# Sums of output weight blocks, made in the prompt's output stage and read back by the sample's

## The chip, the cores and the metric

The kernel runs on one core of a Trainium2 chip. The metric is device time in microseconds of one execution, and the median over runs is compared. TensorE (PE in the profile) multiplies matrices, VectorE (DVE) and GpSimd (POOL) work on elements, ScalarE (ACT) applies functions and copies, and SyncE (SP) issues the transfers between DRAM and the on-chip memory (SBUF). Results of TensorE land in PSUM, in 8 banks.

## The reference

One encoder layer is applied with the same weights to two batches, the prompt (512 tokens) and the sample (1024 tokens), 1024 channels wide, all in float32.

```python
def encoder_layer(x, norm_g, w_in, ..., w_o_a, w_o_b, w_out, t5_table):
    h = rmsnorm(x, norm_g)
    proj = h @ w_in
    qa, ka, va, za, qb, kb, vb, zb, ga, gb = jnp.split(proj, ..., axis=-1)
    ...
    oa = neighbourhood_attention(qa, ka, va, rpb_a) * jax.nn.silu(za)
    oa = oa @ w_o_a
    ...
    ob = window_gqa_attention(qb, kb, vb, t5_table, sink_b) * jax.nn.silu(zb)
    ob = ob @ w_o_b
    merged = jax.nn.sigmoid(ga) * oa + jax.nn.sigmoid(gb) * ob
    return x + merged @ w_out
```

This case is about the last line, merged @ w_out, for the prompt and for the sample.

## The kernel before

**Matrix products.** Every float32 factor is split into a high and a low part (`split`: ScalarE makes the high part, VectorE or GpSimd the low one as a difference), and a product is three matmuls: high by high, high by low, low by high (lines 1288, 1289 and 1290). A weight tile of 128 x 512 holds four blocks of 128 x 128, that is four steps over k, so one `product` of a weight tile is 12 matmuls of 512 columns.

**Stages.** The order is: prompt attention, prompt dense stages, sample attention, sample dense stages. A dense phase runs through the gate products, the merge, and at last the output stage, which takes the 8 chunks of w_out's columns in 4 pairs. A pair has four raw weight tiles, written (m, j): chunk m of the pair, half j of k.

**The prompt's output stage** uses `pair_classic` (line 1312): for each chunk of a pair it loads two raw tiles (`load_raw`, line 1250), splits them (`weight_tiles`, line 1255), and makes two products into one bank. `post_out` (line 1566) adds x and stores y.

**The sample's output stage** uses Strassen-Winograd products on the pair, 7 products for 8, in `pairs_apart` (line 1401). They need sums of the weight tiles: s1 = (1,0) + (1,1), s2 = s1 - (0,0), s3 = (0,0) - (1,0), s4 = (0,1) - s2. A first loop over the four pairs loads the four raw tiles, makes the four sums in tiles named S, stores s1, s2 and s3 in DRAM (`s_d`, line 1430), and computes three products, with (0,0), (0,1) and s4. A second loop loads s1, s2 and s3 again (line 1452) along with the raw tile (1,1), and computes the other four. The first loop's weights are prepared while the merge (`merged_sums` and the lines around it) is still running.

**What sets the order.** A planner (`Flow.run`) works when the program is built. It simulates the engines with costs in nanoseconds, takes on each engine the ready operation of the lowest priority number, and so fixes the order in which each engine, and the DMA queue, gets its instructions. An addition of two SBUF tiles (`tt`, line 1161) may go to VectorE or GpSimd; the planner charges 602 ns on the one and 1249 ns on the other, and takes the engine that would be done first, with a bias. On the chip each engine then goes through its list and waits on semaphores.

**Rings.** A tile of a ring (`room`, line 233) is given out when the tile that many places before it is free, that is when every operation that names it is done. The rings of `IN_TURN` (line 153) are given out strictly in the order of the program. Those that matter here: "raw" (4 tiles, for loaded weights), "whi" and "wlo" (6 each, for split weights; the attention weights of the sample come next in the same rings), "S" (3, in the sample only), "C" (x and y).

**The hand-over.** The sample's attention opens its late tiles (line 1849) only when the pools of the prompt's output stage are released; "raw" and "C" are in them.

Of the kernel before, what the change touches and what calls it, by code (L numbers as in the profile page):

```python
# [10 lines left out]
F32 = mybir.dt.float32  # L11
F32R = mybir.dt.float32r
AF = mybir.ActivationFunctionType
ALU = mybir.AluOpType
# [26 lines left out]
P = 128  # L41
# [313 lines left out]
def encoder_kernel(  # L355
# [23 lines left out]
    nc = tc.nc  # L379
# [22 lines left out]
    r_d = dpool.tile([NT_S // P, P], F32, tag="r_d", name="r_d")  # L402
    t_d = dpool.tile([4, 4, P, NT_S // 2], F32, tag="t_d", name="t_d")
    o_d = {geo.nt: dpool.tile([2, 8, P, geo.nt], F32, tag=f"o_d{geo.nt}", name=f"o_d{geo.nt}") for geo in (gp, gs)}

    def expand(geo, h, lo):

# [728 lines left out]
    def dense_phase(geo, hh, hl, h_ops, o_stores, exps_done, start, opened, tp, up, p0, p1, p2, x_t, y_t, classic, fill, after_gates=None, side=None):  # L1136
# [3 lines left out]
        nh = 512  # L1140
# [3 lines left out]
        short = nt == nh  # L1144
# [2 lines left out]
        g_d = dpool.tile([2, 8, P, nt], F32, tag=f"g_d{nt}", name=f"g_d{nt}")  # L1147
        p_d = None if short else dpool.tile([2, 4, P, sn], F32, tag="p_d", name="p_d")
        m_d = None if short else dpool.tile([4, 4, P, sn], F32, tag="m_d", name="m_d")
        s_d = None if short else dpool.tile([8, 3, P, nh], F32, tag="s_d", name="s_d")  # L1150
        stores = {}
        h_reads = []
        tags = iter(ROTA * 50)
# [155 lines left out]

            return mov  # L1310

        def pair_classic(srcs, post, prio, mov_h, after=lambda i: ()):

            i = 0
            for m, src in enumerate(srcs):
                ws = weight_tiles([load_raw(src[j], prio - 2) for j in range(2)], 4, prio)
                for n in halves:
                    ps = bank(next(tags))
                    o = product(ps, ws[0], mov_h(0, n), prio, True, False, after(i))
                    h_reads.append(product(ps, ws[1], mov_h(1, n), prio, False, True, [o]))  # L1320
                    i += 1
                    post(m, n * nh, nh, ps, True, prio)
# [78 lines left out]
        def pairs_apart(jobs, prio, mov_h, mov_t, late, seed=None, ready=()):  # L1401

            kept = []

            def take(ps, w, mov, pr, first, last, after=(), again=False, n=sn):
                o = product(ps, w, mov, pr, first, last, [*after, *ready], n, again)
                h_reads.append(o)
                return o
# [3 lines left out]
                    (("act", ACT_(sn, False)),), lambda e: act.activation(out.t, ps.t[:, :sn], AF.Copy), pr, new=[out], use=[ps],  # L1412
                )

            for i, (at, srcs, post) in enumerate(jobs):
                pr = prio + i / 8
                raw = {(m, j): load_raw(srcs[m][j], pr - 2) for m, j in ((0, 0), (1, 0), (1, 1), (0, 1))}
                s1, s2, s4, s3 = (tile_("S", 3, 512) for _ in range(4))
                saves = []
                for j, out, in0, in1, op in (  # L1420
                    (2, s1, raw[1, 0], raw[1, 1], ALU.add), (0, s2, s1, raw[0, 0], ALU.subtract),
                    (None, s4, raw[0, 1], s2, ALU.subtract), (1, s3, raw[0, 0], raw[1, 0], ALU.subtract),
                ):
                    tt(
                        lambda out=out: out.t, lambda in0=in0: in0.t, lambda in1=in1: in1.t, op, 512,
                        pr - 0.5 + (j == 1), new=[out], use=[in0, in1],
                    )
                    if j is not None:
                        saves.append(dma(
                            lambda j=j, out=out, at=at: nc.sync.dma_start(s_d[at, j], out.t), 262144, pr, use=[out],  # L1430
                        ))
                w = weight_tiles([raw[0, 0], raw[0, 1], s4], 6, pr - 0.5)
                p1, c = (spare(t) for t in (("fr", "fl"), ("fr", "fl"), ("fh", "fc"), ("fh", "w32"))[i])
                ps, p7 = bank(next(tags)), bank(next(tags))
                take(ps, w[0], mov_h(0, 0), pr, True, True)
                o = leave(p1, ps, pr)
                take(p7, w[2], mov_h(1, 1), pr, True, True)
                if seed:
                    seed(i)(0, sn, sn, None, pr, c, ready)
                    tt(lambda c=c: c.t[:, :sn], lambda c=c: c.t[:, :sn], lambda p7=p7: p7.t[:, :sn], ALU.add, sn, pr, psum=True, use=[c, p7], into=[c])  # L1440
                else:
                    leave(c, p7, pr)
                take(ps, w[1], mov_h(1, 0), pr, False, True, [o], True)
                post(0, 0, sn, ps, True, pr)
                kept.append((p1, c, saves))

            for i, ((at, srcs, post), (p1, c, saves)) in enumerate(zip(jobs, kept)):
                pr = late + i
                raw = []
                for j in range(3):  # L1450
                    v = tile_("raw", 4, 512)
                    dma(lambda v=v, j=j, at=at: nc.sync.dma_start(v.t, s_d[at, j]), 262144, pr - 2, new=[v], after=saves)
                    raw.append(v)
                w = weight_tiles([*raw, load_raw(srcs[1][1], pr - 2)], 6, pr - 0.5)
                pv = lambda v: (lambda: v.t[:, :sn])

                def mul(j, t):
# [286 lines left out]
        mov_h = blocks(m_ops, nh)  # L1744
        if not short:
            jobs = [
                (4 + i, [[w_out[c, j] for j in range(2)] for c in (2 * i, 2 * i + 1)], lambda m, *a, i=i: post_out(2 * i + m, *a))
                for i in range(4)
            ]
            seeds = lambda i: lambda m, *a: with_x(2 * i + m, *a)  # L1750
# [3 lines left out]
        for i in range(4):  # L1754
            srcs = [[w_out[c, j] for j in range(2)] for c in (2 * i, 2 * i + 1)]
            post = lambda m, *a, i=i: post_out(2 * i + m, *a)
            if i < o_classic:
                pair_classic(srcs, post, 20 + i, mov_h)
            else:
                seed = lambda m, *a, i=i: with_x(2 * i + m, *a)  # L1760
                pair_strassen(srcs, post, 20 + i, mov_h, mov_t, seed, i == 3)
# [180 lines left out]
```

## Time and profile before

| What | Value |
|---|---|
| three runs | 1134.73, 1137.67, 1137.1 us; median 1137.1 |
| the profiled execution | 1136.88 us, its span 1135.1 us |
| granted TensorE clock | 1.00 over nearly all of the span |
| transfers | 186.11 MB, 164 GB/s in the mean |
| prompt's output stage, TensorE | 351.1 to 394.6 us from the start of the span |
| sample's output stage, TensorE | 1054.6 to 1131.9 us |

The profile shows one execution. Times in its rows count from the start of the span. A group's row gives the engine, the source line, the operation, the tile written and the tiles read, and how often; L1164 is the addition in `tt`, L1170 and L1175 are the two halves of `split`. A matmul's busy time (0.39 us for 512 columns) overlaps the next matmul's, so the start-to-start distance is what a matmul costs.

### The profile page before, as it was taken

The numbers are of one execution on the slowest core, as the hardware profiler recorded it, in microseconds if no ns is written. First come the engines' busy times: TensorE is split into PE (matmuls) and PEld (weight loads), VectorE is DVE, ScalarE is ACT, GpSimd is POOL, SyncE is SP. The second block draws the span as 40 slices with busy tenths as digits, with TensorE's granted clock in tenths as the row PEclk, the third lists the DMA queues.
The fourth block names the chain that finished last, engine by engine and source line by source line (L and its number), as shares of the span: only waits on it lengthen the run. The fifth ranks groups of instructions, "written<-read, shape, count | busy, mean of one in ns | idle before, by whom it ended". The sixth has DMA issues, their size and how long they took to land.

```text
span 1135.1 us, 18686 instructions
## 1 busy us (share of the span) xinstructions
PE 1121.6 (99%) x6079; PEld 973.9 (86%) x6079; DVE 863.8 (76%) x1995; ACT 653.7 (58%) x1498; POOL 327.1 (29%) x432
## 2 busy tenths in 40 slices
PE   8999999999999999999999999999999999999998
PEld 6999988888888889999899988988788888788887
DVE  5888797587765468887868888885888866779874
ACT  6777987644433246574759888876534434522440
POOL 4654433000010044433414344420033221124221
PEclk9999999999999999999999999999999999999999
DMA  7854533488786422121312314244958645868982
GB/s 261 273 157 139 183 115 103 110 262 260 241 276 196 159 91 72 29 79 29 91 32 84 82 38 112 57 131 127 300 187 244 218 167 180 297 219 281 302 279 93
DMA packets 139108, 186.11 MB, mean 164 GB/s; under 512 B 29897, under 2 KB 68561, under 8 KB 139010
## 3 DMA queue, kind: packets, MB, share of 16 engines
q1 hardware_dynamic: 139010, 184.91, 51.4%
q8 instruction: 48, 0.79, 0.3%
q14 instruction: 50, 0.41, 0.1%
HBM read 138.71 MB, written 50.88 MB: 167 GB/s over the span
## 4 chain that ended last, share of the span: by engine, by line
PE 89%; DMA 4%; DVE 4%; ACT 1%; issue 1%; SPq 0%; POOL 0%; DVEq 0%; POOLq 0%; ACTq 0%
PE p L761 25%; PE x L1288 8%; PE x L1290 8%; PE x L1289 8%; PE x L1063 5%; PE x L1026 5%; PE x L934 5%; PE d L1288 4%; PE d L1289 4%; PE d L1290 4%; PE p L1289 4%; PE p L1290 4%; PE p L1288 4%; PE x L861 2%; DMA ot<-u_d 1%
## 5 line engine op out<-in xcount | busy, mean ns | idle before, releaser
L761 PE MATMUL p<-whi,hh 128*128 128x384 f32 x384 | 133.6, 348 | 0.0
L761 PE MATMUL p<-whi,hl 128*128 128x384 f32 x384 | 132.4, 345 | 0.0
L761 PE MATMUL p<-wlo,hh 128*128 128x384 f32 x384 | 132.2, 344 | 0.0
L978 ACT ACTIVATE sb<-sb,mx 128x384 f32<-128x384 f32 (+1 forms) x192 | 107.7, 565 | 22.9 <-DVE mx L969 22.6
L1170 ACT ACTIVATE whi<-raw 128x512 fp32r<-128x512 f32 (+1 forms) x136 | 79.4, 599 | 67.4 <-PE x L1289 46.3
L1289 PE MATMUL x<-T,whi 128*128 128x512 f32 x284 | 110.7, 390 | 0.3 <-DVE T L1175 0.2
L1288 PE MATMUL x<-T,whi 128*128 128x512 f32 x284 | 110.6, 390 | 0.0
L1290 PE MATMUL x<-T,wlo 128*128 128x512 f32 x284 | 110.5, 389 | 0.0
L761 PE MATMUL p<-whi,hb 128*128 128x384 f32 x384 | 107.8, 346 | 0.0
L1037 DVE TENSOR_TENSOR pp<-x,pp 128x512 fp32r<-128x512 f32 (+1 forms) x136 | 82.6, 639 | 20.3 <-ACT pp L1032 19.2
L1175 DVE TENSOR_TENSOR wlo<-raw,whi 128x512 fp32r<-128x512 f32 (+1 forms) x109 | 73.3, 682 | 26.5 <-ACT whi L1170 26.0
L1175 POOL TENSOR_TENSOR wlo<-raw,whi 128x512 fp32r<-128x512 f32 (+1 forms) x27 | 32.1, 1199 | 172.9 <-ACT whi L1170 160.2
L799 POOL TENSOR_TENSOR rs_r<-rs_v,mhalf 128x4 f32<-128x4 f32 (+1 forms) x72 | 79.9, 1109 | 5.7
L1032 ACT ACTIVATE pp<-x 128x512 fp32r<-128x512 f32 (+1 forms) x136 | 70.9, 561 | 18.2 <-PE x L1026 17.1
L792 POOL TENSOR_SCALAR rs_v<-ss 128x4 f32<-128x4 f32 (+1 forms) x72 | 26.0, 361 | 185.1 <-DVE ss L785 181.7
L1063 PE MATMUL x<-pp,v 128*128 128x256 f32 (+1 forms) x368 | 76.6, 322 | 0.0
L1288 PE MATMUL x<-hh,whi 128*128 128x512 f32 x196 | 76.4, 390 | 0.1
L1290 PE MATMUL x<-hh,wlo 128*128 128x512 f32 x196 | 76.3, 389 | 0.0
L1289 PE MATMUL x<-hl,whi 128*128 128x512 f32 x196 | 76.2, 389 | 0.0
L761 PEld LDWEIGHTS p<-whi,hl 128*128 128x128 f32 x384 | 72.8, 190 | 1.3 <-issue 1.0
L761 PEld LDWEIGHTS p<-whi,hh 128*128 128x128 f32 x384 | 73.0, 190 | 1.1 <-issue 0.5
L761 PEld LDWEIGHTS p<-wlo,hh 128*128 128x128 f32 x384 | 72.9, 190 | 0.9 <-issue 0.5
(381 smaller groups left out, 3011.9 us busy)
## 6 DMA issues: line engine op xcount, KB each, us to landing
raw<-in_w_g_dram SPq DMA_DIRECT2D x84, 256.0 KB
w<-in_w_att_dram SPq DMA_DIRECT2D x46, 384.0 KB
raw<-in_w_z_dram SPq DMA_DIRECT2D x40, 256.0 KB
ot<-o_d SPq DMA_DIRECT2D x36, 256.0 KB
raw<-in_w_out_dram SPq DMA_DIRECT2D x36, 256.0 KB
g_d<-C SPq DMA_DIRECT2D x34, 256.0 KB
fr<-in_w_g_dram SPq DMA_DIRECT2D x28, 256.0 KB
out_dram<-C SPq DMA_DIRECT2D x19, 256.0 KB
```

The costliest lines, as they stand in the source:

```text
L761: pe.matmul(ps.t[:, :GW], part[u](k), mv.t[:, c], start=k == 0 and m == 0, stop=k == KC - 1 and m == 2,)
L799: lambda e: nc.gpsimd.tensor_tensor(r.t[:, :nn], rv.t[:, :nn], mhalf[:, :nn], op=ALU.pow),
L934: pe.matmul(pss[2 * pair + i].t[:, :width], q.t[rows, u, at : at + P], kv[:, tiles[0] : tiles[-1] + 1 : step], start=n == 0, stop=n == 2,)
L978: act.activation(sb.t[:, :width], sb.t[:, :width], AF.Exp, bias=mx.t[:, i : i + 1], scale=-1.0, accum_out=sm.t[:, i : i + 1],)
L1032: lambda e, pt=pt, pp=pp, nn=nn: act.activation(pp.t[:, 0, :nn], pt.t[:, :nn], AF.Copy),
L1037: lambda e, pt=pt, pp=pp, nn=nn: dve.tensor_tensor(pp.t[:, 1, :nn], pt.t[:, :nn], pp.t[:, 0, :nn].bitcast(F32), op=ALU.subtract),
L1063: pe.matmul(out(), v.t[:, vs], mv(), start=first, stop=last)
L1170: (("act", ACT_(n)),), lambda e: act.activation(hi(), src(), AF.Copy), prio,
L1175: lambda e: engines[e].tensor_tensor(lo(), src(), hi().bitcast(F32), op=ALU.subtract), prio,
L1288: pe.matmul(out, hi.t[:, cs], mh(), start=first and k == 0, stop=False, **more)
L1289: pe.matmul(out, hi.t[:, cs], ml(), start=False, stop=False, **more)
L1290: pe.matmul(out, lo.t[:, cs], mh(), start=False, stop=last and k == len(ws) - 1, **more)
```

## The change

The sums move to the prompt's output stage. `weight_sums` is called there once per pair, after the pair's last split is planned. It waits for all of the pair's splits and then makes the four sums in a chain, each one in place of a raw tile that has been split: s1 into (1,1), s3 into (1,0), s2 into (0,0), s4 into (0,1). Each is stored in `s_d`, which is now one DRAM tile for the whole kernel and holds four sums a pair.

In the sample, the first loop loads (0,0), (0,1) and s4, and the second s1, s2, s3 and (1,1). No S tiles are made there and nothing is stored in `s_d`. A load of a sum waits for its own store only.

```diff
+    s_d = dpool.tile([4, 4, P, 512], F32, tag="s_d", name="s_d")
+    s_saves = {}
...
-        s_d = None if short else dpool.tile([8, 3, P, nh], F32, tag="s_d", name="s_d")
...
-        def pair_classic(srcs, post, prio, mov_h, after=lambda i: ()):
+        def weight_sums(i, raw, ends, prio):
+            o = None
+            for j, out, in0, in1, op in (
+                (2, (1, 1), (1, 0), (1, 1), ALU.add), (1, (1, 0), (0, 0), (1, 0), ALU.subtract),
+                (0, (0, 0), (1, 1), (0, 0), ALU.subtract), (3, (0, 1), (0, 1), (0, 0), ALU.subtract),
+            ):
+                v, a, b = raw[out], raw[in0], raw[in1]
+                o = tt(
+                    lambda v=v: v.t, lambda a=a: a.t, lambda b=b: b.t, op, 512, prio, hold=[v, a, b],
+                    after=[*ends, *([o] if o else [])],
+                )
+                s_saves[i, j] = dma(
+                    lambda v=v, j=j: nc.sync.dma_start(s_d[i, j], v.t), 262144, prio, after=[o], hold=[v],
+                )
+
+        def pair_classic(srcs, post, prio, mov_h, after=lambda i: (), sums_of=None):
             i = 0
+            raws, ends = {}, []
             for m, src in enumerate(srcs):
-                ws = weight_tiles([load_raw(src[j], prio - 2) for j in range(2)], 4, prio)
+                raws.update({(m, j): load_raw(src[j], prio - 2) for j in range(2)})
+                ws = weight_tiles([raws[m, j] for j in range(2)], 4, prio)
+                ends += [x for w in ws for *_, ops in w for x in ops]
+                if m and sums_of is not None:
+                    weight_sums(sums_of, raws, ends, prio + 0.5)
...
+            def load_sum(i, j, prio):
+                v = tile_("raw", 4, 512)
+                dma(lambda: nc.sync.dma_start(v.t, s_d[i, j]), 262144, prio - 2, new=[v], after=[s_saves[i, j], start])
+                return v
...
-            for i, (at, srcs, post) in enumerate(jobs):
+            for i, (srcs, post) in enumerate(jobs):
                 pr = prio + i / 8
-                raw = {(m, j): load_raw(srcs[m][j], pr - 2) for m, j in ((0, 0), (1, 0), (1, 1), (0, 1))}
-                s1, s2, s4, s3 = (tile_("S", 3, 512) for _ in range(4))
-                saves = []
...
-                w = weight_tiles([raw[0, 0], raw[0, 1], s4], 6, pr - 0.5)
+                w = weight_tiles([load_raw(srcs[0][0], pr - 2), load_raw(srcs[0][1], pr - 2), load_sum(i, 3, pr)], 6, pr - 0.5)
...
-            for i, ((at, srcs, post), (p1, c, saves)) in enumerate(zip(jobs, kept)):
+                kept.append((p1, c))
+
+            for i, ((srcs, post), (p1, c)) in enumerate(zip(jobs, kept)):
                 pr = late + i
-                raw = []
-                for j in range(3):
-                    v = tile_("raw", 4, 512)
-                    dma(lambda v=v, j=j, at=at: nc.sync.dma_start(v.t, s_d[at, j]), 262144, pr - 2, new=[v], after=saves)
-                    raw.append(v)
-                w = weight_tiles([*raw, load_raw(srcs[1][1], pr - 2)], 6, pr - 0.5)
+                w = weight_tiles([*(load_sum(i, j, pr) for j in range(3)), load_raw(srcs[1][1], pr - 2)], 6, pr - 0.5)
...
-                pair_classic(srcs, post, 20 + i, mov_h)
+                pair_classic(srcs, post, 20 + i, mov_h, sums_of=i)
```

More of the change, by code (lines that the diff above doesn't have):

```diff
@@ L1413, in leave @@
                 )
-            for i, (at, srcs, post) in enumerate(jobs):
+            for i, (srcs, post) in enumerate(jobs):
                 pr = prio + i / 8
-                raw = {(m, j): load_raw(srcs[m][j], pr - 2) for m, j in ((0, 0), (1, 0), (1, 1), (0, 1))}
-                s1, s2, s4, s3 = (tile_("S", 3, 512) for _ in range(4))
-                saves = []
[L1420 to L1431, printed above, removed]
-                w = weight_tiles([raw[0, 0], raw[0, 1], s4], 6, pr - 0.5)
+                w = weight_tiles([load_raw(srcs[0][0], pr - 2), load_raw(srcs[0][1], pr - 2), load_sum(i, 3, pr)], 6, pr - 0.5)
                 p1, c = (spare(t) for t in (("fr", "fl"), ("fr", "fl"), ("fh", "fc"), ("fh", "w32"))[i])
@@ L1444, in pairs_apart @@
                 post(0, 0, sn, ps, True, pr)
-                kept.append((p1, c, saves))
-            for i, ((at, srcs, post), (p1, c, saves)) in enumerate(zip(jobs, kept)):
+                kept.append((p1, c))
+            for i, ((srcs, post), (p1, c)) in enumerate(zip(jobs, kept)):
                 pr = late + i
-                raw = []
-                for j in range(3):
-                    v = tile_("raw", 4, 512)
-                    dma(lambda v=v, j=j, at=at: nc.sync.dma_start(v.t, s_d[at, j]), 262144, pr - 2, new=[v], after=saves)
-                    raw.append(v)
-                w = weight_tiles([*raw, load_raw(srcs[1][1], pr - 2)], 6, pr - 0.5)
+                w = weight_tiles([*(load_sum(i, j, pr) for j in range(3)), load_raw(srcs[1][1], pr - 2)], 6, pr - 0.5)
                 pv = lambda v: (lambda: v.t[:, :sn])
@@ L1746, in dense_phase @@
             jobs = [
-                (4 + i, [[w_out[c, j] for j in range(2)] for c in (2 * i, 2 * i + 1)], lambda m, *a, i=i: post_out(2 * i + m, *a))
+                ([[w_out[c, j] for j in range(2)] for c in (2 * i, 2 * i + 1)], lambda m, *a, i=i: post_out(2 * i + m, *a))
                 for i in range(4)
```

## The prediction

> **What bounds the kernel now.** I read the page's busy times first, then a table of stretches around the two output stages, then single rows there.
>
> ```profile
> span 1135.1 us, 18686 instructions
> ...
> PE 1121.6 (99%) x6079; PEld 973.9 (86%) x6079; DVE 863.8 (76%) x1995; ACT 653.7 (58%) x1498; POOL 327.1 (29%) x432
> ```
>
> TensorE is busy in 1121.6 of 1135.1 us, so 13.5 us of idle time is all that any change of waiting can give back, and the change leaves every matmul in place. A busy share can hide slow matmuls, so the next view, the busy time of each engine in chosen stretches, puts counts beside it.
>
> ```profile
> core 0: us, PE busy (x) PEld busy (x) DVE busy (x) ACT busy (x) POOL busy (x), PEclk, DMA share, GB/s
> ...
> 351.10:394.60 43.50, 43.50 (x193) 36.03 (x193) 18.53 (x26) 11.84 (x18) 0.00 (x0) 1.00 0.49 166
> 394.60:410.00 15.40, 14.24 (x82) 13.61 (x82) 8.86 (x21) 6.94 (x15) 4.44 (x6) 1.00 0.59 192
> 1023.50:1054.60 31.10, 31.10 (x139) 25.76 (x138) 29.42 (x39) 9.31 (x18) 15.05 (x11) 1.00 0.81 279
> 1054.60:1131.90 77.30, 77.11 (x349) 63.48 (x348) 52.77 (x82) 24.05 (x45) 13.80 (x13) 1.00 0.66 227
> ```
>
> The first row is the prompt's output stage: 8 column chunks of 24 matmuls, 192 in 43.5 us, so 0.2266 us from one start to the next, without a gap. The last row is the sample's output stage: 28 products of 12 matmuls, 336 of full width (two half products stand for the last), which at 0.2266 take 76.1 us; the stretch has 77.3. So 1.2 us is the most that a better sample's output stage can give. The third row, the merge ahead of it, is where the sums are made now: VectorE is busy in 29.4 of 31.1 us, but TensorE has no gap at all. Two of the gaps in the stage can be seen in TensorE's timeline, where the next matmul starts 0.45 and 0.49 us after the one before in place of 0.23:
>
> ```profile
> 1059.40 0.39 PE L1288 MATMUL p<-hh,whi 128*128 128x512 f32 x1
> 1059.85 0.50 PE L1289 MATMUL p<-hl,whi 128*128 128x512 f32 x1
> ...
> 1076.53 0.39 PE L1290 MATMUL x<-hh,wlo 128*128 128x512 f32 x1
> 1077.02 0.50 PE L1288 MATMUL x<-hh,whi 128*128 128x512 f32 x1
> ```
>
> They are worth 0.22 and 0.26 us.
>
> **What the change takes out of the sample's stage.** The instructions that make the tiles S, and the DMAs to and from s_d:
>
> ```profile
> L1164 DVE TENSOR_TENSOR S<-raw x6: 674/685/694, 1024.9 to 1068.0; 128x512 f32<-128x512 f32 x6
> ...
> L1164 POOL TENSOR_TENSOR S<-S,raw x3: 1294/1616/1677, 1025.7 to 1050.5; 128x512 f32<-128x512 f32 x3
> L1164 DVE TENSOR_TENSOR S<-raw,S x3: 678/1780/1782, 1027.8 to 1052.3; 128x512 f32<-128x512 f32 x3
> L1164 POOL TENSOR_TENSOR S<-raw x2: 1571/1670/1770, 1027.9 to 1040.7; 128x512 f32<-128x512 f32 x2
> L1164 DVE TENSOR_TENSOR S<-S,raw x1: 686/686/686, 1062.5 to 1062.5; 128x512 f32<-128x512 f32 x1
> L1164 POOL TENSOR_TENSOR S<-raw,S x1: 1298/1298/1298, 1063.3 to 1063.3; 128x512 f32<-128x512 f32 x1
> ```
> ```profile
> L1430 SPq DMA_DIRECT2D s_d<-S x12: 319/320/522, 1025.6 to 1071.8; - x12
> L1452 SPq DMA_DIRECT2D raw<-s_d x12: 319/320/1433, 1069.1 to 1098.7; - x12
> ```
>
> 16 sums go: 10 on VectorE (6 x 0.685 + 3 x 1.78 + 0.69, about 10 us) and 6 on GpSimd (3 x 1.62 + 2 x 1.67 + 1.30, about 9.5 us). 12 stores go. The first loop loads 3 tiles a pair in place of 4; the second still loads 4, but no longer waits for stores of its own stage. All of this lies beside a TensorE that is full, so it pays only through the gaps: between 0 and 1.2 us. I take 0.4, the two gaps above less a little, since the second is near the reading back of s_d, which now is written hundreds of microseconds earlier, and the first is not.
>
> **What it adds to the prompt's stage.** 16 sums, 4 a pair in a chain, and 16 stores of 256 KB. The instructions are cheap; what counts is that each sum is made in place of a raw tile, so that the ring of 4 raw buffers, which before came free one by one after each split, now is held by one pair until its sums are stored. So I follow one turn of that ring. The rows, by view (the chain of waits; raw tiles from 348.5 us on; VectorE's, ScalarE's and the DMA queue's timeline; the waits of that queue, with their sum, count and longest; stretches of half a microsecond):
>
> ```profile
> 351.08 0.23 PE x L1288
> ...
> 393.93 3.90 DMA fr<-in_w_g_dram
> ```
> ```profile
> L1175 DVE TENSOR_TENSOR wlo<-raw,whi x13: 682/684/694, 348.5 to 378.9; 128x512 fp32r<-128x512 f32 x13
> ```
> ```profile
> 348.53 0.69 DVE L1175 TENSOR_TENSOR wlo<-raw,whi 128x512 fp32r<-128x512 f32 x1 [1.44 <-ACT whi L1170]
> ...
> 357.16 0.68 DVE L1175 TENSOR_TENSOR wlo<-raw,whi 128x512 fp32r<-128x512 f32 x1
> ...
> 394.63 0.69 DVE L1164 TENSOR_TENSOR C<-p,C 128x512 f32<-128x512 f32 x1 [1.11 <-PE p L1290]
> ```
> ```profile
> 356.38 0.63 ACT L1170 ACTIVATE whi<-raw 128x512 fp32r<-128x512 f32 x1 [2.09 <-PE x L1289]
> ```
> ```profile
> 373.60 0.34 SPq L1575 DMA_DIRECT2D out_dram<-C  x1
> 375.63 0.33 SPq L1561 DMA_DIRECT2D C<-in_xt_p_dram  x1
> ...
> 395.35 0.34 SPq L1575 DMA_DIRECT2D out_dram<-C  x1
> ...
> 400.94 0.43 SPq L671 DMA_DIRECT2D mask<-in_mask_s_dram  x1
> ```
> ```profile
> SPq L1561 <- DMA out_dram<-C: 4.7, 4, 1.7
> ```
> ```profile
> 377.50:378.00 0.50, 0.50 (x4) 0.42 (x3) 0.00 (x0) 0.00 (x0) 0.00 (x0) 1.00 0.38 143
> 378.00:378.50 0.50, 0.50 (x4) 0.42 (x3) 0.19 (x1) 0.41 (x1) 0.00 (x0) 1.00 0.00 0
> ```
>
> When TensorE needs each pair: the stage starts at 351.08 and its last result is added at 394.63, so a chunk takes 5.44 us and a pair 10.88. Pair 0 starts at 351.08, pair 1 at 361.96, pair 2 at 372.84, pair 3 at 383.72.
>
> When pair 0's tiles may be summed: there are 16 splits, of which 13 remain from 348.5 on, so the first of these is the fourth, pair 0's last. It ends at 348.53 + 0.69 = 349.22. Before, the rest were split as the ring of 6 weight tiles came free (the 2.09 before the ScalarE row is a wait for TensorE), 13 us ahead of use; this lead is the cover under which the new chain must fit.
>
> One turn, from the end T of a pair's last split: the sums take 0.69 each on VectorE, so the third, on which the oldest buffer waits, ends at T + 2.1 and the fourth at T + 2.8. A store takes about 2.0 (issued 373.60; the queue, which waited for it, goes on at 375.63). So the first load of the next pair is issued at T + 4.2. A load: the one issued at 375.63 has no bytes moving after 378.0, so 2.4 at least; 3.9 for the row of fr, which had a second one behind it. The split takes 1.46 (ScalarE from 356.38, VectorE to 357.84). So the next pair's first operand is ready at T + 8.1 to T + 9.6, and its fourth, three loads later at 0.6 us each (the spacing at which the queue issues, nearly twice the 0.33 of an issue) to 0.94 (262 KB at the 279 GB/s of the merge's row above), at T + 9.9 to T + 12.4.
>
> So pair 1 is ready at 357.3 to 358.8, and later by up to 1.8 where pair 0's sums take turns with the last merges' three adds on VectorE: 1.4 to 4.7 us ahead of 361.96. A turn of 9.9 to 12.4 stands against TensorE's 10.88, so each further pair gains 1.0 or loses 1.5. Pair 3's lead is then between -1.6 and +6.7. The stall is 0 to 1.6 us; I take 0, since the middle (turn 11.15, lead 3.0) leaves 2.5.
>
> VectorE has 18.5 of 43.5 us in use there; 16 x 0.69 = 11.0 more makes 29.6. The 16 stores are 4.2 MB, 96 GB/s on top of 166, so the DMA share goes from 0.49 to about 0.77. On the DMA queue, which issues in order, the stores wait for VectorE, and behind them stand the loads of x and the stores of y. An add that comes late for that holds one of 8 PSUM banks, each good for 5.44 us, so TensorE doesn't notice. Attention weights for the sample take their turn behind pair 3's in the weight tiles; with pair 3 split by about 385 they are still 9 us ahead of 394.6.
>
> **The sum.** 1136.88 (the profiled execution; its span is 1135.1, and it is 0.2 below the median 1137.1 of the three runs) + 0 for the prompt's stage - 0.4 for the sample's = 1136.5. A change below 0.3%, 3.4 us, can't be told from none by a measurement of this kernel, whose three runs are 2.9 us apart.
>
> **Rivals.** *The ring turns too slowly: slower.* The place is the second and third turn, the price a TensorE stall before pairs 1 to 3. It needs a turn above 10.88 by more than half the first lead. Sums on GpSimd would do it: 1.30 each in place of 0.69, so the third at T + 3.9 and the fourth at T + 5.2; the first operand is ready at T + 9.9 to 11.4, the fourth at T + 12.4 to 14.5. With the short ends nothing is lost but 0.2 us before pair 3; with the long ones pair 1 is late by 0.5, pair 2 by 3.6 more, pair 3 by 3.6 more, 7.7 in all. The middle is 3.9, so 1140.4. For it: 6 of the 16 sums now run on GpSimd. Against it: they do where VectorE is full, while in the prompt's stage GpSimd does nothing (0.00, x0) though 12 splits may go there. A sum on GpSimd may also slow VectorE:
>
> ```profile
> 1040.68 1.57 POOL L1164 TENSOR_TENSOR S<-raw 128x512 f32<-128x512 f32 x1 [0.74 <-DMA s_d<-S]
> ```
> ```profile
> 1041.02 1.78 DVE L1164 TENSOR_TENSOR S<-raw,S 128x512 f32<-128x512 f32 x1
> ```
>
> The VectorE sum that overlaps it takes 1.78 in place of 0.69, 1.1 more, which would come on top once a pair. The Trainium skill, page "SBUF — State Buffer", section "SBUF: two separate sides", gives the reason as an exclusive lock: a VectorE operation with two inputs in SBUF and a GpSimd operation that reads SBUF don't overlap, the second waits. By that rule a GpSimd sum stalls the splits outright and the long end grows by about 3 us; this row agrees.
>
> *The hand-over waits.* The sample's mask is loaded at 400.94, once the prompt's last tiles are free, which before is when the store issued at 395.35 has landed, at 397.4. If pair 3's last sum lands after that, attention starts late, at most by the 2.0 of a store: 1138.5, within the bound. Against it: pair 3's sums end near 388.
>
> *The relief pays more.* If TensorE ran faster beside less DMA and VectorE traffic, the time would fall. The Trainium skill, page "Perfetto Trace Analysis", section "Identifying the Most-Contended Engine", says that matmul busy time is no measure of headroom and that weight loads are; by it 63.5 of 77.3 us would leave 18% open in the last stretch. The spacing says otherwise: 0.2266 us in the prompt's stage at a DMA share of 0.49, and 31.1 us for 139 matmuls (those cut by the edges counted) at 0.81. The most is 1.2 us there and what idle time elsewhere a new order of work happens to close, 1.2 of it at 394.6 to 410: 1134.5, which is still within the bound; to pass it, a new order would have to close more of the 13.5 us.
>
> **Chances.** Forecast 0.66, slow ring 0.24, late hand-over 0.06, more relief 0.04. The slow ring runs from 0.2 to 7.7 us, and I put two thirds of it past the bound; of the relief, half. So faster 0.02, same 0.82, slower 0.16. The range goes from 1134.5 (the relief's end, and close to the lowest run, 1134.73) to 1141.5, which holds the slow ring's middle and 1.1 more.
>
> **What would show it.** Right: 16 sums on VectorE and 16 stores from raw tiles between 349 and 391 us, TensorE at 0.2266 per matmul through 394, the sample's output stage with no S and one gap less. Wrong: TensorE gaps of over 1 us before a pair's first matmul in the prompt's stage, ended by a weight split that waited for a load of w_out that waited for an s_d store; sums on GpSimd there; or a sample's output stage shorter than 76 us.

## The result and the profile after

The changed kernel is slower: a median of 1138.78 us in 21 runs (1135.01 to 1142.29) against 1135.40 in 21 runs of the kernel before (1132.89 to 1137.67), a ratio of 1.0029 with an interval of 1.0022 to 1.0036. That is 3.3 us, between 2.5 and 4.1. The time lies inside the range of the prediction, but its sum, 1136.5 us, had a gain of 0.4. In a second set of runs the same kernel came out at 1.0037 (1.0025 to 1.0049).

The profiled execution took 1137.66 us, only 0.8 above that of before. It lies in the lower half of its kernel's runs and the profile of before in the upper half of its own, so the two profiles show less than the difference of the medians. I therefore read a second profile of the changed kernel beside the first (experiment e1, 1139.74 us).

The page's head, then the four stretches of the prediction (the same columns), then the tile s_d:

```profile
span 1135.9 us, 18696 instructions
...
PE 1121.8 (99%) x6079; PEld 972.7 (86%) x6079; DVE 864.3 (76%) x1993; ACT 652.0 (57%) x1499; POOL 327.7 (29%) x433
```
```profile
351.10:394.60 43.50, 42.55 (x186) 34.26 (x185) 23.75 (x36) 10.45 (x16) 5.68 (x4) 1.00 0.73 243
394.60:410.00 15.40, 14.37 (x79) 13.04 (x77) 10.80 (x21) 7.41 (x14) 5.23 (x6) 1.00 0.82 288
1023.50:1054.60 31.10, 31.10 (x139) 25.75 (x138) 24.97 (x32) 10.17 (x19) 10.95 (x9) 1.00 0.67 215
1054.60:1131.90 77.30, 76.01 (x344) 62.98 (x343) 48.79 (x74) 22.58 (x44) 13.93 (x13) 1.00 0.58 194
```
```profile
L1326 SPq DMA_DIRECT2D s_d<-raw x16: 319/320/327, 349.9 to 393.5; - x16
L1429 SPq DMA_DIRECT2D raw<-s_d x16: 320/326/1473, 1021.3 to 1099.6; - x16
```

The change does what it says: 16 stores of sums between 349.9 and 393.5 us, 16 loads of them in the sample. The merge before the sample's output stage is relieved, as VectorE's 25.0 us against 29.4 show, and TensorE was full there already. But TensorE, which had no gap in the prompt's output stage, now idles 0.95 us there and 1.03 us in the stretch behind it, where it idled 1.16 us before.

Why, the chain of waits says. In this view each row is what the row after it waited for (start, us, what), so it can be read from the end backwards. Before, this chain runs through TensorE alone up to 391.4. After, it looks like this between 350 and 410 us:

```profile
350.74 1.68 POOL raw L1166
...
355.16 0.70 DVE hl L1177
...
356.64 0.33 SPq L1254
...
357.02 4.60 DMA raw<-in_w_out_dram
...
363.02 0.70 DVE wlo L1177
...
365.79 2.04 DMA out_dram<-C
...
368.83 4.66 DMA raw<-in_w_out_dram
...
374.88 1.31 DVE wlo L1177 x2
...
382.08 4.33 DMA raw<-in_w_out_dram
...
387.81 0.70 DVE wlo L1177
...
389.15 0.96 DVE wlo L610
390.13 3.56 DMA w<-in_w_att_dram
...
395.66 3.57 DMA w<-in_w_att_dram
...
402.65 5.01 DMA mask<-in_mask_s_dram
...
409.74 0.44 PE x L864 x2
```

Three things are to be seen. First, TensorE is not in it until 409.74: the stage runs on the speed at which tiles are loaded, split, summed and stored. Second, one turn of the ring of raw tiles, from a pair's last low part to the next pair's: 376.19 - 363.72 = 12.5 and 388.51 - 376.19 = 12.3, against TensorE's 10.88. Pair 0's last split is the first row of the next fence; it ends at 348.67, so the first turn took 15.0.

```profile
347.98 0.69 DVE L1177 TENSOR_TENSOR wlo<-raw,whi 128x512 fp32r<-128x512 f32 x1 [1.12 <-ACT whi L1172]
```
```profile
350.74 1.67 POOL L1166 TENSOR_TENSOR raw<-raw 128x512 f32<-128x512 f32 x1 [3.90 <-DVE raw L1166]
365.38 1.29 POOL L1166 TENSOR_TENSOR raw<-raw 128x512 f32<-128x512 f32 x1 [12.97 <-DVE raw L1166]
376.26 1.29 POOL L1166 TENSOR_TENSOR raw<-raw 128x512 f32<-128x512 f32 x1 [9.60 <-DVE wlo L1177]
390.92 1.79 POOL L1166 TENSOR_TENSOR raw<-raw 128x512 f32<-128x512 f32 x1 [13.37 <-DVE raw L1166]
```

One sum of each pair went to GpSimd, 1.29 to 1.79 us in place of 0.69 (the fence above is GpSimd's timeline, all four rows that it has between 347 and 395 us). Third, what makes the next pair's raw loads late is their place in the in-order DMA queue. In the queue's own waits between 349 and 406 us no raw load (L1254) waits for a store to land, so its buffer was free by the time it was its turn. Ahead of the raw loads stand the stores of the sums, which wait for the sums, and loads of x, one of which waits for hl until 355.86 in the first turn (sum, count, longest):

```profile
SPq L1326 <- DVE raw L1166: 10.6, 12, 3.8
SPq L1568 <- DVE hl L1177: 2.0, 2, 1.8
```

In the second turn the chain names the store of y at 365.79, which landed at 367.83. It cost 0.1 us at most, since the queue was busy with the stores of the sums until 367.74 (two, issued from 366.69 on, 1.05 us).

The end of the chain is the sample's. The first six weight tiles of its attention come through a ring of two ("w"), so a load waits until the tile two places earlier is split: the load at 390.13 was issued when the low part made at 389.15 was done. ScalarE could start on them only at 387.69, behind pair 3's last high part, while before it split them from 380.81 on, one for each weight tile that TensorE gave back. The sixth split stands in ScalarE's timeline of before and after, with what ended the wait:

```profile
394.41 0.85 ACT L602 ACTIVATE whi<-w 128x768 fp32r<-128x768 f32 x1 [1.87 <-PE p L1289]
```
```profile
401.55 0.85 ACT L605 ACTIVATE whi<-w 128x768 fp32r<-128x768 f32 x1 [0.85 <-DMA w<-in_w_att_dram]
```

It is 7.1 us later and now waits for a transfer. Behind the last low parts stands, on VectorE, the split of a gate weight (fl), behind that the loads of the next ones, and behind those the mask, which is issued at 402.65 in place of 400.94.

What TensorE waited for between 345 and 412 us (us in total, times, longest), in the profiles of before, after and after again:

```profile
PE x L861 <- DVE qk L816: 1.1, 1, 1.1
```
```profile
PE x L864 <- DVE qk L819: 1.0, 1, 1.0
PE p L1290 <- ACT whi L1172: 0.9, 1, 0.9
```
```profile
PE x L864 <- DVE qk L819: 1.8, 1, 1.8
PE p L1290 <- ACT whi L1172: 0.8, 1, 0.8
PE x L1290 <- ACT hh L1172: 0.4, 1, 0.4
PE x L1291 <- DVE hl L1177: 0.2, 1, 0.2
```

The wait for whi is pair 3's first weight (384.11 on ScalarE, 384.79 on TensorE), the wait for qk is the attention's start, and hh is the activation's split at the start of the stage. In the sample's output stage the two small gaps of before are gone, and one that is larger has come, where a copy on ScalarE stands behind a split that waits for a transfer (TensorE's timeline, after):

```profile
1085.99 0.50 PE L1290 MATMUL x<-hh,whi 128*128 128x512 f32 x1 [1.29 <-ACT fh L1439]
```

### The profile page after: what moved, and what is told of

The parts are those of the page before. It is cut to its first block, busy times and chain, and to the rows that moved or that the text cites. A ratio compares the mean times of both kernels' runs of the same rounds, so it can differ in the third digit from the quotient of the medians.

```text
span 1135.9 us, 18696 instructions
## 1 busy us (share of the span) xinstructions
PE 1121.8 (99%) x6079; PEld 972.7 (86%) x6079; DVE 864.3 (76%) x1993; ACT 652.0 (57%) x1499; POOL 327.7 (29%) x433
## 4 chain that ended last, share of the span: by engine, by line
PE 87%; DMA 6%; DVE 3%; issue 2%; ACT 1%; SPq 1%; POOL 0%; ACTq 0%; DVEq 0%; POOLq 0%
PE p L764 25%; PE x L1291 8%; PE x L1290 8%; PE x L1292 8%; PE x L1066 5%; PE x L937 5%; PE x L1029 5%; PE d L1290 4%; PE p L1291 4%; PE p L1292 4%; PE p L1290 4%; PE d L1291 4%; PE d L1292 4%; PE x L864 2%; DMA raw<-in_w_out_dram 1%
## 5 line engine op out<-in xcount | busy, mean ns | idle before, releaser
L1177 DVE TENSOR_TENSOR wlo<-raw,whi 128x512 fp32r<-128x512 f32 (+1 forms) x111 | 77.1, 706 | 34.4 <-ACT whi L1172 32.0
L1177 POOL TENSOR_TENSOR wlo<-raw,whi 128x512 fp32r<-128x512 f32 (+1 forms) x29 | 34.7, 1207 | 198.5 <-DMA raw<-in_w_g_dram 111.6
L764 PEld LDWEIGHTS p<-whi,hb 128*128 128x128 f32 x384 | 69.1, 188 | 3.0 <-issue 1.3
```

Source lines behind the costliest of these rows:

```text
L764: pe.matmul(ps.t[:, :GW], part[u](k), mv.t[:, c], start=k == 0 and m == 0, stop=k == KC - 1 and m == 2,)
L1177: lambda e: engines[e].tensor_tensor(lo(), src(), hi().bitcast(F32), op=ALU.subtract), prio,
```

## The experiments

My theory after the two profiles (lateness): the added sums and stores make the ring turn slowly, pair 3 comes late, and with it all that follows it in the queue and on ScalarE and VectorE up to the attention's start. The rival (order): the planner sees other costs in the prompt's output stage and lays out all later work differently, and that new order costs the time wherever it happens to be worse. A second rival asks whether sums or stores are the cost. Times are medians with the ratio to the kernel before and its interval; differences in us are the ratios times 1135.

**e1, the changed kernel again.** No edit.

> The changed kernel once more, for a second profile and time. Both theories: 2.6 to 4.1 us above before. Theory ring (the raw tiles are held through sums and stores, the next pair's weights come late): TensorE loses 2 us or more between 351 and 396 us, and that is more than half of the difference. Theory sample (the new order of work in the sample's output stage makes a wait of its own): TensorE loses under 1 us in the prompt's stage and 2 us or more between 1055 and 1133.

1139.74 us, 1.0037 (1.0025 to 1.0049). The slowdown is there again, with more of it in the profile: TensorE idle for 3.2 us between 351.1 and 410.0 (the four waits of the last fence but one), where the first profile had 2.0 and before 1.2.

**e2, the prompt's half alone.** The kernel before, with the 16 sums and stores in the prompt, into a tile that nobody reads. The sample makes its own sums as before.

```diff
+    q_d = dpool.tile([4, 4, P, 512], F32, tag="q_d", name="q_d")
+        def weight_sums(i, raw, ends, prio):
...
-                pair_classic(srcs, post, 20 + i, mov_h)
+                pair_classic(srcs, post, 20 + i, mov_h, sums_of=i)
```

> The prompt's stage makes and stores the 16 sums, but nobody reads them; the sample makes its own as before. Theory ring: 2 to 4 us above before. Theory sample: within 1 us of before. A third theory, that the planner's new order costs time in the sample's attention, would show as lost TensorE time between 410 and 800 here.

1138.12 us, 1.0019 (1.0009 to 1.0029).

**e3, the sample's half alone.** The prompt as before; the sample's new loops load raw tiles of w_out where the sums would be, so the sums are left out of what it computes.

```diff
-                dma(lambda: nc.sync.dma_start(v.t, s_d[i, j]), 262144, prio - 2, new=[v], after=[s_saves[i, j], start])
+                dma(lambda: nc.sync.dma_start(v.t, w_out[2 * i + j // 2, j % 2]), 262144, prio - 2, new=[v], after=[start])
...
-                pair_classic(srcs, post, 20 + i, mov_h, sums_of=i)
+                pair_classic(srcs, post, 20 + i, mov_h)
```

> The prompt's stage as before, without sums; the sample has the new two loops, but loads raw tiles of w_out where the sums would be read, so the sums are left out of the computation. Theory ring: between 1 us below before and the same. Theory sample: 2 to 3.5 us above before.

1136.38 us, 1.0005 (0.9995 to 1.0014). The loss is in the prompt's half, and the sample's half alone gains nothing that can be measured. TensorE's matmuls come in e3's trace in the order of before, so the two can be laid side by side: from the matmul that starts at 1050.11 us before (1049.35 in e3) to the last one e3 takes 0.2 us less.

**e4, six raw buffers.** In pairs 1 and 3 the first two raw tiles go into the idle ring of gate weights ("fr"), and so need not wait for a store.

```diff
-                raws.update({(m, j): load_raw(src[j], prio - 2) for j in range(2)})
+                more = sums_of in (1, 3) and not m
+                new = lambda: (spare("fr"), m_ops[5, 0]) if more else ()
+                raws.update({(m, j): load_raw(src[j], prio - 2, *new()) for j in range(2)})
```

> The change with two more buffers in the prompt's output stage: the first two raw tiles of pairs 1 and 3 go into the ring fr, which is idle there, so that these weights don't wait for the sums of the pair before. Theory ring: 1 us below to 1 us above before, with under 0.5 us lost in the prompt's stage. Theory sample: 2 to 3.5 us above before, as the change itself.

1140.62 us, 1.0039 (1.0027 to 1.0052). Lateness had this one come back towards before, and it didn't. The profile says why only in part. The wait before pair 3 is gone, but the attention's start waits longer (TensorE's waits, 345 to 412 us):

```profile
PE x L864 <- DVE qk L819: 2.8, 1, 2.8
PE x L1290 <- ACT hh L1172: 0.3, 1, 0.3
PE x L1291 <- DVE hl L1177: 0.2, 1, 0.2
```

The planner had laid out all work anew for it, and from here on I suspected the order more. The traces don't bear that out for TensorE: by tiles and shapes its 6079 matmuls come in the order of before. Only the other engines and the queue have another one.

**e5 and e6, two pairs in the prompt, two in the sample.** MADE names the pairs whose sums the prompt makes; for the others the sample makes them as before.

```diff
+    MADE = (0, 1)
...
+                if i in MADE:
+                    first = [load_raw(srcs[0][0], pr - 2), load_raw(srcs[0][1], pr - 2), load_sum(i, 3, pr)]
+                else:
+                    first = sums_here(i, srcs, pr)
```

> Sums of pairs 0 and 1 are made in the prompt's stage, those of pairs 2 and 3 in the sample's as before. Theory lateness (the ring's turns push the last weights of the prompt, and behind them the attention weights and the gate weights of the sample, so that TensorE loses time before pair 3 and again at the hand-over between 396 and 412 us): within 1 us of before, since pairs 2 and 3 release their buffers one by one and catch up. Theory traffic (every sum and store added there costs alike): half of the change, 1.2 to 2.2 us above before.

> The other half: sums of pairs 2 and 3 in the prompt's stage, those of 0 and 1 in the sample's as before. As many sums and stores are moved as with pairs 0 and 1. Theory lateness: 2 to 4 us above before, lost at the hand-over and before pair 3. Theory traffic: 1.2 to 2.2 us above before.

Pairs 0 and 1: 1138.22 us, 1.0020 (1.0005 to 1.0035). Pairs 2 and 3: 1137.92 us, 1.0029 (1.0018 to 1.0039). Neither half is free. In e5 TensorE's order is that of before, and in e6 it is but for 2 of 6079 matmuls, so their losses of 2.3 and 3.3 us aren't due to TensorE's order. e6's profiled execution was one of its fastest and shows no new wait.

**e7 and e8, sums alone, stores alone.** e2 without the stores; e2 without the sums, with the raw tiles stored as they are.

```diff
-                dma(
-                    lambda v=v, j=j: nc.sync.dma_start(q_d[i, j], v.t), 262144, prio, after=[o], hold=[v],
-                )
```
```diff
-                o = tt(
-                    lambda v=v: v.t, lambda a=a: a.t, lambda b=b: b.t, op, 512, prio, hold=[v, a, b],
-                    after=[*ends, *([o] if o else [])],
-                )
```

> As the prompt half, but the 16 sums are not stored (nobody reads them; the sample makes its own). A turn of the ring is 2 us shorter. Theory lateness: no loss before pair 3, and 0 to 1 us above before. Theory traffic: near before, as the stores are gone. So this run tells only whether the sums by themselves cost.

> As the prompt half, but the 16 raw tiles are stored as they are after the pair's splits, without sums (nobody reads them; the sample makes its own). A turn is 2.8 us shorter than with sums. Theory lateness: 0 to 1 us above before. Theory traffic: 1.5 to 2.5 us above before, like the prompt half.

Sums alone: 1143.90 us, 1.0083 (1.0065 to 1.0101). Stores alone: 1140.40 us, 1.0045 (1.0031 to 1.0059). Each part costs more than both together in e2. That can hardly be the cost of the parts. TensorE has an order of its own here: 4287 of its 6079 matmuls stand in the same place as before in e7, 4381 in e8 and 5290 in the changed kernel. So the order had to be taken out of the comparison.

**e9, the order alone.** The sums and stores are planned, with their costs, holds and waits, but not issued. TensorE and ScalarE get the changed kernel's order to the last instruction. The sample loads raw tiles for sums, as in e3.

```diff
-                o = tt(
-                    lambda v=v: v.t, lambda a=a: a.t, lambda b=b: b.t, op, 512, prio, hold=[v, a, b],
-                    after=[*ends, *([o] if o else [])],
-                )
+                o = f.op(any_tt(512), lambda e: None, prio, hold=[v, a, b], after=[*ends, *([o] if o else [])])
...
-                    lambda v=v, j=j: nc.sync.dma_start(s_d[i, j], v.t), 262144, prio, after=[o], hold=[v],
+                    lambda: None, 262144, prio, after=[o], hold=[v],
```

> The changed kernel's order of work on every engine, with its 16 sums and 16 stores planned but not issued; the sample loads raw tiles of w_out where it would read sums, so the sums are left out of the computation. Theory lateness (the sums and stores themselves delay the weights in the prompt's stage): within 1 us of before, and no loss between 351 and 412 us beyond that of before. Theory order (the change costs because the planner puts all later work in another order, with luck of its own): 2 to 4 us above before, as the change.

1135.16 us, 0.9983 (0.9971 to 0.9996): 1.9 us faster than before. The order theory falls for this change: the changed kernel's order, together with the sample's relief, is a gain. What the issued sums and stores cost is then 1.0029 / 0.9983 = 1.0046, or 5.2 us, give or take 1.6 (the two intervals combined). The profile of e9 has the two stretches full:

```profile
351.10:394.60 43.50, 43.50 (x194) 36.02 (x193) 19.16 (x28) 11.40 (x17) 0.00 (x0) 1.00 0.52 177
394.60:410.00 15.40, 15.40 (x89) 14.88 (x88) 10.92 (x25) 7.34 (x15) 5.74 (x7) 1.00 0.67 223
```

Since all 6079 matmuls come in one order, the same two can be found in each trace: the first of the prompt's output stage, and one behind the attention's start (TensorE's timeline, e9, then after).

```profile
351.18 0.39 PE L1290 MATMUL x<-hh,whi 128*128 128x512 f32 x1
...
425.04 0.64 PE L1066 MATMUL x<-pp,v 128*128 128x256 f32 x4
```
```profile
350.73 0.39 PE L1290 MATMUL x<-hh,whi 128*128 128x512 f32 x1
...
427.89 0.64 PE L1066 MATMUL x<-pp,v 128*128 128x256 f32 x4
```

From the one to the other e9 takes 73.86 us and the changed kernel 77.16, 3.30 more. In e1's profile (350.61 and 430.77) it is 6.30 more, and up to the last matmul the two are 2.79 and 5.00 behind. So the loss of 5.2 lies here, and nothing is added to it later. It comes at three places. Before pair 3 TensorE falls 1.5 us behind e9, 1.4 in e1's profile, and at the attention's start 1.5 and 3.7. The rest, 0.4 and 1.2, comes within pair 0, where e1's trace has it wait for hh and hl; e3's profile, without any sum in the prompt, loses 1.1 there against before, so that part isn't shown to be the sums' doing.

The kernel of e2 has the changed kernel's TensorE order too. It is at 1.0019 / 0.9983 = 1.0036 of e9, 4.1 us, give or take 1.8, which agrees.

**e10, e7's order alone.** The same for e7: sums planned, nothing issued, everything computed.

```diff
-                o = tt(
-                    lambda v=v: v.t, lambda a=a: a.t, lambda b=b: b.t, op, 512, prio, hold=[v, a, b],
-                    after=[*ends, *([o] if o else [])],
-                )
+                o = f.op(any_tt(512), lambda e: None, prio, hold=[v, a, b], after=[*ends, *([o] if o else [])])
```

> The order of the run with sums alone, 9 us above before, with its 16 sums planned but not issued. What is computed is what the kernel before computes. Theory order: 7 to 10 us above before, lost after 600 us where that run lost it. Theory lateness: within 1 us of before.

1142.67 us, 1.0058 (1.0039 to 1.0076). Of the 9.4 us that e7 lost, 6.6 are its order, 450 us away from the sums: in the stretch from 800 to 1000 us TensorE starts 20 matmuls fewer than before (first e10, then before).

```profile
800.00:1000.00 200.00, 195.14 (x848) 159.32 (x847) 159.00 (x243) 91.90 (x177) 50.33 (x43) 0.99 0.72 233
```
```profile
800.00:1000.00 200.00, 198.40 (x868) 162.29 (x867) 156.08 (x236) 86.52 (x164) 49.39 (x43) 1.00 0.69 227
```

**e11 and e12, a nudge.** The kernel before, with 300 or 1000 ns of TensorE time at the end of the prompt's output stage that only the planner sees. The chip gets the same instructions.

```diff
+                    if short and prio == 23 and m:
+                        f.op((("pe", 300),), lambda e: None, prio, after=h_reads[-1:])
```

> The kernel before, with 300 ns of TensorE time at the end of the prompt's output stage that only the planner sees: the same instructions, in another order from there on. Theory order: 1 us or more away from before, in either direction. Theory lateness: within 0.7 us.

> As the run with 300 ns, with 1000 ns. Theory order: 1 us or more away from before, and another distance than with 300 ns. Theory lateness: within 0.7 us.

300 ns: 1139.28 us, 1.0026 (1.0016 to 1.0036). 1000 ns: 1142.00 us, 1.0048 (1.0030 to 1.0067). An edit that adds no work at all costs 3.0 and 5.4 us. So the plan of before was a lucky one next to these and to e10's, though not next to that of e9, and e7 and e8 hold such a term of unknown size. In e3 to e6 it can't come from TensorE's order, which is that of before (but for e6's 2 matmuls); what the new order of the other engines and of the queue does there isn't known. Only kernels with one and the same order tell the parts apart.

**f1 to f3 and f5, parts with the order held.** All use the changed kernel's plan and leave out the issue of some of it, and where a sum isn't made or stored the sample loads a raw tile in its place. f1 issues the sums and no stores, f2 the stores (of raw tiles) and no sums, f3 both for pairs 0 to 2, f5 both for pair 3 only.

```diff
-                    lambda v=v, j=j: nc.sync.dma_start(s_d[i, j], v.t), 262144, prio, after=[o], hold=[v],
+                    lambda: None, 262144, prio, after=[o], hold=[v],
```
```diff
+                if i in (0, 1, 2):
+                    o = tt(
...
+                else:
+                    o = f.op(any_tt(512), lambda e: None, prio, hold=[v, a, b], after=[*ends, *([o] if o else [])])
```

> The changed kernel's order; the 16 sums are made, but not stored, and the sample loads raw tiles of w_out where it would read sums, so the sums don't enter the result. Theory ring (a turn of the raw ring is sums, store, load, split, and too long): a turn is 2 us or more shorter, no stall before pair 3, 1.5 us below before to 0.5 above. Theory engines (the sums take VectorE and GpSimd from the merges and from the attention's start): 1.5 to 3.5 us above before, as the change.

> The changed kernel's order; 16 stores are made, of the raw tiles as they are, without the sums, and the sample reads these, so the sums are left out of the computation. Theory ring: a turn is 2.8 us or more shorter, 1.5 us below before to 0.5 above. Theory queue (16 stores in the one DMA queue delay the attention's and the gates' weights behind them): 1.5 to 3.5 us above before, lost at the hand-over.

> The changed kernel's order, without the sums and stores of pair 3; the sample loads raw tiles of w_out for that pair's sums, which are left out of the computation. Theory ring: pair 3 still waits for pair 2's sums, so 1 us or more is lost before it, and the hand-over, whose weights come behind pair 3's, loses as in the change: 1.5 to 3.3 us above before. Theory queue: the hand-over is relieved, within 1 us of before.

> The changed kernel's order, with the sums and stores of pair 3 alone; the sample loads raw tiles of w_out for the sums of pairs 0 to 2, which are left out of the computation. Theory ring (only a chain of late turns brings pair 3's work into the hand-over): the turns before are short, pair 3 is split in time, 2 us below before to the same. Theory last pair (its sums and stores cost at the hand-over whenever they come): 1 to 2.5 us above before, lost between 396 and 412 us.

| Issued, in one order | Median, us | Ratio to before | Above e9, us | Behind e9 in the profile, us |
|---|---|---|---|---|
| nothing (e9) | 1135.16 | 0.9983 (0.9971 to 0.9996) | 0 | 0 |
| sums (f1) | 1133.99 | 0.9997 (0.9985 to 1.0010) | 1.6 | 0.37 |
| stores (f2) | 1134.81 | 0.9991 (0.9979 to 1.0002) | 0.9 | 1.40 |
| pairs 0 to 2 (f3) | 1135.20 | 0.9998 (0.9987 to 1.0008) | 1.7 | 2.35 |
| pair 3 (f5) | 1135.43 | 0.9999 (0.9986 to 1.0012) | 1.8 | 0.73 |
| everything | 1138.78 | 1.0029 (1.0022 to 1.0036) | 5.2 | 3.30 and 6.30 |

The fourth column is a difference of two ratios, each row with about 2 us either way, so no single part is shown to cost anything. The fifth is the time between the two matmuls of e9's fences, in one profile each. Sums and stores together cost 5.2 where alone they give 1.6 + 0.9, and the pairs 1.7 + 1.8. That the whole is more than its parts is what the numbers suggest, the fifth column (0.37 + 1.40) for sums and stores too; within these intervals it isn't shown. TensorE's waits between 345 and 412 us point the same way, in f1, f2, f3 and f5:

```profile
PE x L864 <- DVE qk L819: 0.2, 1, 0.2
```
```profile
PE x L864 <- DVE qk L819: 0.4, 1, 0.4
```
```profile
PE p L1290 <- ACT whi L1172: 0.9, 1, 0.9
PE x L864 <- DVE qk L819: 0.5, 1, 0.5
```
```profile
PE x L864 <- DVE qk L819: 0.3, 1, 0.3
```

With sums alone or stores alone pair 3 shows no wait for whi in these profiles (with stores alone TensorE still falls 0.6 us behind e9 there). Three pairs of both bring the wait before pair 3, and only all four bring the full wait for qk.

**f4, six raw buffers with the order held.** The changed kernel in its own order; two raw tiles of pairs 1 and 3 are placed in "fr".

```diff
+                if sums_of in (1, 3) and not m:
+                    raws[0, 0].place = raws[0, 1].place = wpool, "fr", 2
```

> The whole change with its order of work, but the first two raw tiles of pairs 1 and 3 lie in two idle buffers of the ring fr, so that their loads don't wait for the stores before them to land. Theory ring: a turn is 2 us shorter where it counts, no stall before pair 3, 1 us below before to 1 above. Theories queue and engines: 2 to 3.5 us above before, as the change.

1139.14 us, 1.0025 (1.0011 to 1.0040). Against 1.0029 nothing is gained that can be measured. The DMA queue shows why. These are its rows for the stores before pair 3 and the loads of pair 3's first two tiles, whose buffers were not held by a sum:

```profile
375.73 2.50 SPq L1327 DMA_DIRECT2D s_d<-raw  x4
...
378.79 0.45 SPq L1255 DMA_DIRECT2D fr<-in_w_out_dram  x1
379.76 0.42 SPq L1255 DMA_DIRECT2D fr<-in_w_out_dram  x1
```

They were issued at 378.79, right behind the four stores, because the queue takes its entries in order and the stores were waiting for their sums. The free buffer is of no use there: in this order it is the place in the queue that makes the loads late as much as the ring. Whether loads put ahead of the stores in the queue would take the loss away in this same order wasn't tried.

**f6, a candidate: pairs 0 to 2 in the prompt, pair 3 in the sample,** with a plan of its own (e5's edit with MADE = (0, 1, 2)).

> Sums of pairs 0 to 2 in the prompt's stage, those of pair 3 in the sample's as before, planned anew. By the run with the same sums in the changed kernel's order it should be within 1 us of before, if the order that the planner finds were as good; by the two runs in which only the order changed, that order by itself may add 0 to 6 us. Theory ring: a stall before pair 3 of about 1.4 us, and under 1.5 us lost between 396 and 412.

1140.71 us, 1.0040 (1.0024 to 1.0056). No kernel here that computes everything beats the one before.

## Why the prediction was wrong

**TensorE as the bound, and the most to be gained: right.** It was full in both output stages before, and most of the loads on the other parts came as worked out (DMA share 0.73 in the prompt's stage, forecast 0.77; no S in the sample's output stage; but VectorE 23.8 us, forecast 29.6). The 0.4 us that I put into the sum for the sample's stage did not show in the times: e3 is at 1.0005, with 0.2 us in its profile. The gaps at 1059 and 1076 went, and a wait of 1.29 us (0.6 in e1's profile) came at 1086.

**The turn of the ring: mis-sized, and this is the step that failed first.** The term of the sum that was wrong is the 0 for the prompt's stage; issuing the sums and stores cost 5.2 us. I took three sums of 0.69 on VectorE and forecast 9.9 to 12.4 us a turn, with a stall of 0. It was 15.0, 12.5 and 12.3. Up to a pair's first operand the sum held: pair 1's was ready at 358.53, forecast 357.3 to 358.8, and the three came 9.9, 9.0 and 9.3 us after the split before, forecast 8.1 to 9.6. The sum on GpSimd in each pair, which I had as a rival and argued away with GpSimd's idleness, had a small part in it: the first load was issued 4.9, 4.6 and 4.4 us after that split, forecast 4.2. (The planner sends a sum there when VectorE has something else to do at that moment, not when it is busy on the average.) The term that was mis-sized is the way from the first operand to the fourth: 5.2, 3.4 and 3.1 us, for which I had three times 0.6 to 0.94. In the first turn it comes from something I had called harmless: "on the DMA queue, which issues in order, the stores wait for VectorE, and behind them stand the loads of x and the stores of y". I followed this only to the adds of y, which do have eight banks of cover. I did not follow it to the next pair's raw loads, which stand in the same queue: the first of pair 1 was issued at 353.60, the other three, behind the load of x that waited for hl, from 356.64 on. In the other two turns it is the loads themselves. They took 4.66 and 4.33 us (the rows at 368.83 and 382.08), where I had 2.4 to 3.9 for the first, and they share the transfers with the stores of the sums issued just before, at a DMA share of 0.89 between 364 and 374 us and 0.83 between 376 and 387. That the stores make them slow is argued from these rows; no run shows it.

**"They are still 9 us ahead of 394.6": the step that failed second.** Pair 3 was split by 388.5, not 385, which alone left 6 us. But the attention weights do not follow at the pace of the splits. They come through a ring of two and each load waits for a split, so two tiles take 5.5 us (390.13 to 395.66) and the sixth is split at 401.55. I had read the row where they wait for TensorE, and not asked what they would wait for next.

**The rivals.** I gave the slow ring 0.24 and the late hand-over 0.06, as two different cases, and set the first at 1140.4 through stalls before pairs 1 to 3, the second at 2.0 us through pair 3's sums. In the traces they are one and the same chain. Of the pairs only pair 3 was waited for, 0.9 us by the wait and 1.5 against e9, and as much or more (1.5 and 3.7) came at the attention's start. The mask was late by 1.7 us, not for the last sum (its store was issued by 393.8) but for the gate weights ahead of it in the queue. Of the 0.82 for no change, much rested on summing each cover alone, while all of them were spent by one delay that was handed on. That the range holds 1138.78 is owed to the width given to the slow ring, not to the sum. And a change below 3.4 us, which I said could not be told from none, can be: 21 runs of each kernel gave 0.8 us either way.

**Shown and not shown.** Shown: the changed order isn't the cause (e9), the issued sums and stores cost 5.2 us in that order (4.1 in e2), and the stretch in which TensorE falls behind is from the start of the prompt's output stage to the attention's, 351 to about 428 us. Seen in the traces but not undone by an experiment: the chain through the queue and the attention weights; f4 removed one wait of it only. Open: how much is due to the sums and how much to the stores, where e9's 1.9 us come from (in its profile 1.2 us less idle time at 394.6 to 410 is most of it, and e3, in TensorE's order of before, gained nothing), and where e6 loses its 3.3.

## What to carry to other kernels

When a step makes a buffer be held longer, follow the delay along the in-order queue to everything behind it, up to the next stage's first loads, and ask of each cover whether an earlier delay has spent it already. Where a planner lays out the instructions, an edit changes two things, the work and the order of all later work. Compare with the order held, by planning the work without issuing it, before a few microseconds are put down to the work, and look in the traces whether the order changed at all: here TensorE's had not in e3 to e5. Where two traces have one order, the starts of the same matmuls show in which stretch the time is lost.

## What the runs showed of the hardware that was not expected

Order alone moves this kernel by 3.0 to 6.6 us with the same instructions (e10 to e12), which is more than the 1.2 us that the sample's output stage had to give. The changed kernel's runs spread over 7.3 us (1135.01 to 1142.29) where those of before spread over 4.8. A kernel whose chain runs through transfers showed 2.0 us of idle TensorE in this stretch in one profile and 3.2 in the next, so one profile is not enough to size such a loss. Idle time is also less than what a wait costs: against the same matmuls of e9 these were 3.3 and 6.3 us. Behind the wait of 0.91 us before pair 3 the next three starts are 0.33, 0.39 and 0.34 us apart (384.79, 385.12, 385.51, 385.85) in place of 0.23.
